# A mixer's first norm applied to the projections' results, and the modulation's loads behind the compression's

## The chip, the cores and the metric

One core of one Trainium2 chip runs the whole program. The metric is the device time of one execution in microseconds. The engines are named as the profile names them: PE is TensorE (PEld its loading of weights), DVE is VectorE, ACT is ScalarE, POOL is GpSimd, SP is the engine whose queue issues nearly all DMA transfers here.

## The reference, cut to what matters

The program is one block of a language model (a mixer of sparse attention and linear attention, then a mixture of 32 experts) followed by two layers of a second block that is modulated by two vectors c and c_ctx. What the change touches stands at the start of the first block and in the modulation of the second:

```python
u = rms_norm(h, g_mix)              # x * rsqrt(mean(x * x) + EPS) * g, row by row (256 rows of 1024)
z = u @ w_in                        # 4904 columns: q, k and v of the sparse attention, its gate,
                                    # q, k, v, a low-rank gate and r of the linear attention, two mixing gates
k_cmp = compress_blocks(k_c, cmp_pos_k, cmp_w1_k, ...)   # gelu(flat @ w1 + b1) @ w2 + b2; the same for v
o = o * rsqrt(mean(o * o) + EPS) * norm_g                # of the linear attention, per head
o = o * silu(r)
...
mod = silu(c) @ ada_w[layer] + ada_b[layer]              # second block, two layers, ada_w is 1024 x 3072
mod_c = silu(c_ctx) @ ada_w[layer] + ada_b[layer]
```

The factor rsqrt(mean + EPS) of the norm, called r1 below, is one number for each row of h, so u @ w_in is r1 times (h * g) @ w_in.

## The kernel before

All data are float32; most products are made as three products of halves: a matrix is split into hi (rounded to fp32r by ScalarE) and lo (the rest, subtracted by VectorE or, for every fourth part, by GpSimd), and gmm (L308) issues hi*hi, hi*lo and lo*hi (named after their tiles in the trace: m<-whi,uhi, m<-wlo,uhi, m<-whi,ulo, all L315). Tokens are held as 2 tiles of 128 rows, u transposed as 8 tiles (k) of 128 x 256.

The weights of the projections come through Feed (L178 on): chunks of 256 columns (the first of 280, the fourth of 272) are loaded by SP into three buffers, one called w (every third chunk), two called wst; a buffer is loaded again as soon as its last part is split. A chunk is split in four parts, into five pairs of buffers whi and wlo. The order of the chunks is Z_ORDER (5, 6, 7, 8, 2, 9, 10, 3, 4, 0, 1). Results go to two banks of PSUM called m; a chunk of more than 256 columns takes both.

TensorE's instructions run in the order in which they are written; the other engines' order is made by a scheduler. To write TensorE's order, the parts of the mixer are generators which drive (L144) interleaves by costs and delays that they yield: gla (linear attention), compress, mixer_proj (the projections), and behind them, as a background stream, ada (the modulation). A stream that waits for a name goes on when another has added it to done.

mixer_in (L490) turns h into four banks t, makes the norm's factor from the sums of squares (Newton steps, rsqrt, L352), turns it into a row R for all partitions (turn_rows, L445), and makes u from the banks: a product with g_mix and R on VectorE, hi on ScalarE, lo on GpSimd (L504 to L507). g_mix stands in VT, which VectorE copies at the start. rope_tables makes cos and sin and their copies times 0.125 for q. mixer_proj (L594) takes the results of each chunk out of PSUM, for the most part with one activation on ScalarE; chunk 5, the first, gives the gate (a tanh) and a part of gqk.

we_load (L377) and we_tile (L384) hand out four buffers called we, 1 MB each, in turn, for the modulation's weights (24 loads of ada_w, pieces of 512 x 512), for the compression's first weights w1 (two halves for keys, two for values) and later for the experts'. A load into a buffer waits until what was in it is multiplied. ada (L1468) loads one piece ahead: in each step it issues the next load, then the four matmuls of the piece at hand (L1502, s<-we,scT), then lets ADA_PACE ns pass in drive's account. compress multiplies w1 at L704 (t<-we,mt).

## Time and profile before

| | us |
|---|---|
| median of 3 runs | 1238.26 |
| lowest, highest | 1237.36, 1241.32 |
| the profiled execution | 1239.08 |
| its span | 1237.3 |
| TensorE busy | 1114.7 (90%) |
| VectorE, ScalarE, GpSimd busy | 562.3, 453.3, 192.2 |

The mixer of the first block runs to about 276 us, the routing to about 300, the experts to about 850, the rest is the second block. The rows further down are copied from the page of the profile and from answers on its trace. A row of a timeline has the start in us, the length in us, engine, line, operation, output<-input and a count of merged instructions; in brackets how long the engine stood idle before it and what ended that. SPq is SP issuing a DMA; its length is that of issuing alone.

### The profile page before, as it was taken

The page shows a single profiled execution, that of the slowest core. Times are in us where ns is not written, and L with a number is a line of the kernel's source. Part 1 is how long each engine was busy: PE and PEld are TensorE (multiplying, and loading weights), DVE is VectorE, ACT ScalarE, POOL GpSimd, SP SyncE. Part 2 cuts the span into 40 slices and gives each one's busy share as a digit, 9 for nine tenths or more (in the row PEclk, how much of TensorE's full clock was granted, in tenths as well). Part 3 has the DMA queues.
Part 4 walks back from the last instruction along what each step waited for, and adds up shares of the span by engine and source line. Part 5 has one row for each costly group of instructions (what it writes and reads, how often), then busy time and mean ns, then how long its engine had stood idle before and what let it go on. Part 6 is the DMA issues. An engine that isn't in the chain of part 4 may idle for free. (4 is left out here: it accounts for less than half of the span.)

```text
span 1237.3 us, 19978 instructions
## 1 busy us (share of the span) xinstructions
PE 1114.7 (90%) x7855; PEld 793.0 (64%) x7855; DVE 562.3 (45%) x1401; ACT 453.3 (37%) x1109; POOL 192.2 (16%) x210
## 2 busy tenths in 40 slices
PE   5999999998989998788989899856989997899996
PEld 4868877784635654433456365512877787899996
DVE  5367773553131212423212300103697668776776
ACT  4534554531012101322210200103567553776663
POOL 6134012111000000000000000000311225325231
PEclk9999999997999999999999999998999998999999
DMA  7897659963999999999999999998535156465331
GB/s 251 281 305 258 205 181 334 342 254 144 358 409 388 374 379 376 409 407 403 409 354 399 401 344 370 388 407 303 167 107 163 56 136 144 132 154 132 110 117 64
DMA packets 181562, 337.64 MB, mean 273 GB/s; under 512 B 20053, under 2 KB 113306, under 8 KB 181466
## 3 DMA queue, kind: packets, MB, share of 16 engines
q1 hardware_dynamic: 179946, 333.78, 75.7%
q0 software_dynamic: 1104, 2.45, 0.7%
q8 instruction: 63, 1.03, 0.3%
q14 instruction: 33, 0.27, 0.1%
q10 hardware_dynamic: 416, 0.10, 0.0%
HBM read 331.58 MB, written 4.73 MB: 272 GB/s over the span
## 5 line engine op out<-in xcount | busy, mean ns | idle before, releaser
L1396 PE MATMUL g<-we,xg 128*32 128x512 f32 x624 | 109.8, 613 | 19.8 <-DMA we<-in_w_gate_dram 9.4
L318 ACT ACTIVATE whi<-wst 128x512 fp32r<-128x512 f32 (+1 forms) x158 | 98.4, 629 | 74.7 <-PE m L315 69.1
L218 DVE TENSOR_TENSOR wlo<-wst,whi 128x512 fp32r<-128x512 f32 (+2 forms) x119 | 93.9, 796 | 64.2 <-ACT whi L318 63.6
L315 PE MATMUL m<-whi,uhi 128*128 128x256 f32 (+2 forms) x368 | 109.8, 298 | 2.6 <-ACT uhi L318 1.9
L315 PE MATMUL m<-wlo,uhi 128*128 128x256 f32 (+2 forms) x368 | 105.9, 288 | 2.6 <-POOL wlo L218 2.6
L315 PE MATMUL m<-whi,ulo 128*128 128x256 f32 (+2 forms) x368 | 105.8, 287 | 0.0
L315 PE MATMUL s<-cuT,wst 128*128 128x256 f32 (+1 forms) x368 | 85.6, 385 | 0.7 <-ACT cuT L318 0.7
L315 PEld LDWEIGHTS s<-cuT,wst 128*128 128x128 f32 (+1 forms) x368 | 64.9, 183 | 27.9 <-issue 17.2
L315 PEld LDWEIGHTS m<-whi,uhi 128*128 128x128 f32 x368 | 71.5, 194 | 12.9 <-issue 5.8
L218 POOL TENSOR_TENSOR wlo<-wst,whi 128x512 fp32r<-128x512 f32 (+1 forms) x39 | 52.2, 1339 | 175.9 <-ACT whi L318 134.9
L218 POOL TENSOR_TENSOR wlo<-w,whi 128x512 fp32r<-128x512 f32 (+4 forms) x21 | 28.0, 1334 | 326.0 <-ACT whi L318 291.7
L315 PE MATMUL m<-xhi,whi 128*128 128x256 f32 x256 | 75.6, 295 | 0.0
L315 PEld LDWEIGHTS m<-wlo,uhi 128*128 128x128 f32 x368 | 71.5, 194 | 2.9 <-POOL wlo L218 2.8
L315 PE MATMUL m<-xhi,wlo 128*128 128x256 f32 x256 | 72.4, 283 | 0.0
L315 PE MATMUL m<-xlo,whi 128*128 128x256 f32 x256 | 72.3, 283 | 0.0
L315 PEld LDWEIGHTS m<-whi,ulo 128*128 128x128 f32 x368 | 71.5, 194 | 0.3 <-POOL ulo L507 0.3
L1396 PEld LDWEIGHTS g<-we,xg 128*32 128x32 f32 x624 | 22.6, 111 | 74.2 <-issue 36.3
L318 ACT ACTIVATE whi<-w 128x512 fp32r<-128x512 f32 (+4 forms) x82 | 50.9, 628 | 34.3 <-PE m L315 29.7
L324 DVE SCALAR_TENSOR_TENSOR eo<-d,STw,eo 128x512 fp32r<-128x512 f32 x16 | 12.0, 748 | 99.8 <-ACT eo L318 99.8
L1424 PE MATMUL d<-we,hT 128*32 128x512 f32 x272 | 49.3, 600 | 7.5 <-DMA we<-in_w_down_dram 6.8
L315 PE MATMUL s<-wst,cuT 128*128 128x256 f32 (+1 forms) x256 | 55.1, 366 | 0.0
L315 PEld LDWEIGHTS s<-wst,cuT 128*128 128x128 f32 x256 | 44.5, 196 | 14.2 <-issue 9.2
(613 smaller groups left out, 2520.3 us busy)
## 6 DMA issues: line engine op xcount, KB each, us to landing
we<-in_w_down_dram SPq DMA_DIRECT2D x40, 1024.0 KB
we<-in_w_gate_dram SPq DMA_DIRECT2D x39, 1024.0 KB
we<-in_w_up_dram SPq DMA_DIRECT2D x39, 1024.0 KB
we<-in_ada_w_dram SPq DMA_DIRECT2D x24, 1024.0 KB
wst<-in_c_in_w_dram SPq DMA_DIRECT2D x19, 1024.0 KB
wst<-in_ab_in_w_dram SPq DMA_DIRECT2D x14, 1024.0 KB
wst<-in_w_in_dram SPq DMA_DIRECT2D x13, 1024.0 KB
w<-in_w_up_dram SPq DMA_DIRECT2D x10, 1024.0 KB
```

The source lines that it names most:

```text
L218: (net.nc.gpsimd if pool else net.nc.vector).tensor_tensor(b, src, a, OP.subtract)
L315: mm(out, l, r, start=first and i == 0, stop=last and i == len(ps) - 1, skip_group_check=True)
L318: return self.nc.scalar.activation(out, in_, f, **kw)
L324: return self.nc.vector.scalar_tensor_tensor(out, a, s, b, op0=op0, op1=op1, **kw)
L1396: nc.tensor.matmul(b[32 * e:32 * e + 32, :], xg[:, 2 * j + r, 32 * e:32 * e + 32], v[e // 2][:, e % 2, 512 * r:512 * r + 512], start=j == ...
L1424: nc.tensor.matmul(ds[hf][32 * e:32 * e + 32, :], hT[:, k, 32 * e:32 * e + 32], v[e // 2][:, e % 2, 512 * hf:512 * hf + 512], start=k == 0 ...
```

## The change

Four things:

- mixer_in makes hi directly from the banks t, as h times g_mix (an activation with a scale), and lo as one scalar_tensor_tensor on VectorE; R is gone. The norm's factor is computed in a function of its own, norm1, that is called after the first chunk's matmuls are written; r1 and r1h (half of it) are scales of the activations that take the projections' results out of PSUM. rope_tables is called after the second chunk's matmuls and makes tables times r1 (ccr, sinr). For chunks 9 and 10 (r of the linear attention) silu leaves r1 out, and gla multiplies the factors of its norm by r1 instead.
- compress adds the name w1 once all four loads of its first weights are written.
- ada's first load is behind a wait for w1; it was the first thing that ada did.
- ADA_PACE is 6000 instead of 7500.

```diff
@@ -44,7 +44,7 @@
 UNIT_Q = 5000
 LANES = 3
 NSA_GAP = 0
-ADA_PACE = 7500
+ADA_PACE = 6000
 ROUTE = 3000
 MAGIC = 12582912.0
 HALVES = [(slice(0, 64), slice(64, 128)), (slice(64, 128), slice(0, 64))]
@@ -492,21 +492,27 @@
         b = self.bank(self.pm, "s", 1)
         nc.tensor.transpose(b[:, :8], self.vr[0:8], self.ident[0:8, 0:8])
         self.copy(self.VT[:, 0:8], b[:, :8])
+
         bs = [self.turn_h(k2, 5) for k2 in range(4)]
+        hi = self.t(A, [128, KD, 256], "uhi", dt=F32R)
+        lo = self.t(A, [128, KD, 256], "ulo", dt=F32R)
+        for k in range(KD):
+            s, g = bs[k // 2][:, 256 * (k % 2):256 * (k % 2) + 256], self.vcol("g_mix", k)
+            self.act(hi[:, k], s, AF.Copy, scale=g)
+            self.stt(lo[:, k], s, g, hi[:, k], OP.mult, OP.subtract)
+        self.uT = (hi, lo)
+
+    def norm1(self):
+
+        A = self.A
         xs = self.t(A, [128, 2, D], "mt1")
         ss = self.t(A, [128, 2], "r1ss")
         self.act(xs[:, 0], self.h[:, 0], AF.Square, accum_out=ss[:, 0:1])
         self.stt(xs[:, 1], self.h[:, 1], 1.0, self.h[:, 1], OP.mult, OP.mult, accum_out=ss[:, 1:2])
-        R = self.turn_rows(A, self.rsqrt(A, ss, 2, 1.0 / D), "r1rb", 5)
-        hi = self.t(A, [128, KD, 256], "uhi", dt=F32R)
-        lo = self.t(A, [128, KD, 256], "ulo", dt=F32R)
-        for k in range(KD):
-            t = xs[:, k // 4, 256 * (k % 4):256 * (k % 4) + 256]
-            self.stt(t, bs[k // 2][:, 256 * (k % 2):256 * (k % 2) + 256], self.vcol("g_mix", k), R, OP.mult, OP.mult)
-            self.act(hi[:, k], t)
-            self.nc.gpsimd.tensor_tensor(lo[:, k], t, hi[:, k], OP.subtract)
-        self.uT = (hi, lo)
-        self.rope_tables(self.K)
+        self.r1 = self.t(A, [128, 2], "r1")
+        self.r1h = self.t(A, [128, 2], "r1h")
+        self.copy(self.r1, self.rsqrt(A, ss, 2, 1.0 / D))
+        self.ts(self.r1h, self.r1, 0.5)
 
     def rope_tables(self, A):
         nc = self.nc
@@ -532,8 +538,15 @@
         self.sin = sin
         self.ccq = self.t(A, [128, 2, 64], "ccq")
         self.sinq = self.t(A, [128, 2, 32], "sinq")
-        self.ts(self.ccq, self.cc, 0.125)
-        self.ts(self.sinq, sin, 0.125)
+
+        self.ccr = self.t(A, [128, 2, 64], "ccr")
+        self.sinr = self.t(A, [128, 2, 32], "sinr")
+        for i in range(2):
+            r = self.r1[:, i:i + 1]
+            self.ts(self.ccr[:, i], self.cc[:, i], r)
+            self.ts(self.sinr[:, i], sin[:, i], r)
+        self.ts(self.ccq, self.ccr, 0.125)
+        self.ts(self.sinq, self.sinr, 0.125)
 
     def rope_half(self, out1, out2, ps, nh, cc, sin, pool):
 
@@ -604,7 +617,12 @@
         self.sr = self.t(A, [128, 2, 512], "sr")
         for ci in Z_ORDER:
             yield from self.proj_tok(self.uT, W_IN[ci][1])
+            if ci == Z_ORDER[0]:
+                self.norm1()
+            if ci == Z_ORDER[1]:
+                self.rope_tables(self.K)
             for i, ps in enumerate(self.res):
+                r, rh = self.r1[:, i:i + 1], self.r1h[:, i:i + 1]
                 if ci < 2:
                     s = slice(4 * ci, 4 * ci + 4)
                     self.rope_half(self.qr[:, i, s, 0:32], self.qr[:, i, s, 32:64],
@@ -612,29 +630,30 @@
                                    self.ccq[:, i], self.sinq[:, i], self.K)
                 elif ci == 2:
                     self.act(self.kcd[:, i], ps.rearrange("p (a d) -> p a d", d=64)[:, :, None, :]
-                             .to_broadcast([128, 4, 2, 64]))
+                             .to_broadcast([128, 4, 2, 64]), scale=r)
                 elif ci in (3, 4):
                     br = ci - 3
                     kd_ = self.ksr[:, i, br]
                     self.rope_half(kd_[:, :, 0:32], kd_[:, :, 32:64],
                                    ps[:, 0:128].rearrange("p (h d) -> p h d", d=64), 2,
-                                   self.cc[:, i], self.sin[:, i], self.K)
-                    self.act(self.vsw[:, i, br], ps[:, 128:256])
+                                   self.ccr[:, i], self.sinr[:, i], self.K)
+                    self.act(self.vsw[:, i, br], ps[:, 128:256], scale=r)
                 elif ci == 5:
-                    self.act(self.gate[:, i], ps[:, 0:24], AF.Tanh, scale=0.5)
+                    self.act(self.gate[:, i], ps[:, 0:24], AF.Tanh, scale=rh)
                     self.ts(self.gate[:, i], self.gate[:, i], 0.5, 0.5, OP.mult, OP.add)
-                    self.act(self.gqk[:, i, 0:256], ps[:, 24:280])
+                    self.act(self.gqk[:, i, 0:256], ps[:, 24:280], scale=r)
                 elif ci == 6:
-                    self.act(self.gqk[:, i, 256:512], ps)
+                    self.act(self.gqk[:, i, 256:512], ps, scale=r)
                 elif ci == 7:
-                    self.act(self.gv[:, i, 0:256], ps)
+                    self.act(self.gv[:, i, 0:256], ps, scale=r)
                 elif ci == 8:
-                    self.act(self.gv[:, i, 256:512], ps[:, 0:256])
-                    self.act(self.ga[:, i], ps[:, 256:272])
+                    self.act(self.gv[:, i, 256:512], ps[:, 0:256], scale=r)
+                    self.act(self.ga[:, i], ps[:, 256:272], scale=r)
                 else:
                     o = self.sr[:, i, (ci - 9) * 256:(ci - 8) * 256]
                     th = self.t(A, [128, 256], "th", 1)
-                    self.act(th, ps, AF.Tanh, scale=0.5)
+
+                    self.act(th, ps, AF.Tanh, scale=rh)
                     self.stt(o, th, 1.0, ps, OP.add, OP.mult)
             self.done.add("z%d" % ci)
         self.dump("gqk", self.gqk)
@@ -645,7 +664,7 @@
             for j in range(4):
                 yield from self.proj_tok(self.uT, 256)
                 for i, ps in enumerate(self.res):
-                    self.act(self.mt[br][:, i, 256 * j:256 * j + 256], ps, AF.Tanh, scale=0.5)
+                    self.act(self.mt[br][:, i, 256 * j:256 * j + 256], ps, AF.Tanh, scale=self.r1h[:, i:i + 1])
             if br:
 
                 for half in range(2):
@@ -696,6 +715,8 @@
             for hf in range(2):
                 w1.append((yield from self.we_load(I["cmp_w1_" + n][0][1024 * hf:1024 * hf + 1024]
                                                    .rearrange("(k p) n -> p k n", p=128), 8, 256)))
+            if kv:
+                self.done.add("w1")
             yield (0, 4000)
             b = self.bank(pm, "t", 5)
             for hf, (v, tag) in enumerate(w1):
@@ -1011,6 +1032,8 @@
                 self.act(junk, b[:, 128 * h:128 * h + 128], AF.Square, accum_out=ssq[:, 4 * i + h:4 * i + h + 1])
             yield 2200
         y = self.rsqrt(G, ssq, 8, 1.0 / 128, "rg")
+        for i in range(2):
+            self.ts(y[:, 4 * i:4 * i + 4], y[:, 4 * i:4 * i + 4], self.r1[:, i:i + 1])
         for i in range(2):
             for h in range(4):
                 hs = slice(128 * h, 128 * h + 128)
@@ -1475,7 +1498,6 @@
                 self.I["ada_w_2"][l][512 * hf:512 * hf + 512, 512 * c:512 * c + 512]
                 .rearrange("(k p) n -> p k n", p=128), 4, 512)))
         todo = [(l, c, hf) for l in range(2) for c in range(6) for hf in range(2)]
-        yield from load()
 
         scT = self.t(A, [128, KD, 42], "scT")
         nc.gpsimd.memset(scT, 0.0)
@@ -1489,6 +1511,8 @@
             self.act(th[:, r], self.vcol(n, 0, 8), AF.Tanh, scale=0.5)
             self.stt(th[:, r], th[:, r], 1.0, self.vcol(n, 0, 8), OP.add, OP.mult)
             self.ts(scT[:, :, 10 + r], th[:, r], 0.5)
+        yield from self.wait("w1")
+        yield from load()
         for l in range(2):
 
             sums = self.bank(self.pm, "s", 1)
```

What this makes of the engines' order, at three places. First VectorE at the start, behind the copy of VT (rs.. are the norm's steps, mt is the product that becomes u, wlo the first weights' low half, w their buffer). Before:

```order
L321 TENSOR_TENSOR rsa<-rsa,rsx 128x2
L324 SCALAR_TENSOR_TENSOR rsy<-rsa,rsy 128x2
L332 COPY r1rb<-rsy 128x256
L218 TENSOR_TENSOR wlo<-w_93,whi 128x560
L324 SCALAR_TENSOR_TENSOR mt_137<-t,VT,r1rb 128x256 x8
L218 TENSOR_TENSOR wlo<-w_93,whi 128x560 x2
```

After:

```order
L324 SCALAR_TENSOR_TENSOR ulo<-t,VT,uhi 128x256
L324 SCALAR_TENSOR_TENSOR rsy<-rsa,rsy 128x2
L321 TENSOR_TENSOR rsa<-rsy 128x2
L321 TENSOR_TENSOR rsa<-rsa,rsx 128x2
L324 SCALAR_TENSOR_TENSOR ulo<-t,VT,uhi 128x256 x6
L218 TENSOR_TENSOR wlo<-w_93,whi 128x560
L324 SCALAR_TENSOR_TENSOR ulo<-t,VT,uhi 128x256
L218 TENSOR_TENSOR wlo<-w_93,whi 128x560 x2
L218 TENSOR_TENSOR wlo<-wst,whi 128x512 x2
L324 SCALAR_TENSOR_TENSOR rsy<-rsa,rsy 128x2
```

The first wlo stood ahead of the eight products, and now stands behind seven of the eight lo; the end of the norm's chain has moved behind the first chunk's splits. ScalarE, in the same way, has seven of the eight hi ahead of the first whi; before, two whi stood ahead of the first hi.

Second SP, which issues the loads in this order (w and wst from in_w_in are chunks of the projections, we the modulation's ada_w and the compression's w1, called cmp_w_k and cmp_w_v). Before:

```order
L431 DMA tab<-in_table_dram 128x1424
L386 DMA we<-in_ada_w_dram 128x4x512
L394 DMA w_271<-in_w_in_dram 128x8x272
L394 DMA wst<-in_w_in_dram 128x8x256 x2
...
L386 DMA we<-in_cmp_w_k_dram 128x8x256
L386 DMA we<-in_ada_w_dram 128x4x512
L394 DMA w_817<-in_w_in_dram 128x8x256
L386 DMA we<-in_cmp_w_v_dram 128x8x256 x2
L386 DMA we<-in_ada_w_dram 128x4x512 x3
```

After:

```order
L431 DMA tab<-in_table_dram 128x1424
L394 DMA w_209<-in_w_in_dram 128x8x272
L394 DMA wst<-in_w_in_dram 128x8x256 x2
...
L386 DMA we<-in_cmp_w_v_dram 128x8x256
L394 DMA w_776<-in_w_in_dram 128x8x256
L386 DMA we<-in_ada_w_dram 128x4x512 x5
L394 DMA wst<-in_w_in_dram 128x8x256
```

The first modulation load was ahead of the fourth chunk's; now it stands behind all four of w1 and behind the tenth chunk's (w_817 before, w_776 after).

Third TensorE where the compression multiplies the keys' w1 (L704 before, L725 after; la and gqk belong to the linear attention). Before:

```order
L925 MATMUL t<-tab,la 128x256 x2
L1502 MATMUL s<-we,scT 32x512 x4
L704 MATMUL t<-we,mt_235 32x256 x8
L437 MATMUL t<-tab,gqk 128x128 x4
L947 MATMUL t<-la,tab 128x256
L704 MATMUL t<-we,mt_235 32x256 x8
```

After:

```order
L946 MATMUL t<-tab,la 128x256 x2
L725 MATMUL t<-we,mt_173 32x256 x16
L437 MATMUL t<-tab,gqk 128x128 x4
L968 MATMUL t<-la,tab 128x256
L1526 MATMUL s<-we,scT 32x512 x4
```

The modulation piece before this place was the fourth; the one after it is the first, and the buffer of its weights is the one that the first eight matmuls of L725 read.

## Rows read from the trace of the kernel before

**Rows 1.** Busy time by stretch (us; instructions), then TensorE's granted clock, DMA share, GB/s:

```profile
16.00:276.00 260.00, 251.82 (x2054) 209.00 (x2054) 150.56 (x379) 129.54 (x325) 64.34 (x66) 0.99 0.79 270
...
20.00:30.00 10.00, 7.38 (x46) 6.96 (x46) 4.85 (x7) 4.49 (x9) 6.95 (x6) 0.84 0.74 271
...
130.00:140.00 10.00, 10.00 (x74) 9.03 (x73) 7.33 (x28) 4.95 (x21) 0.00 (x0) 0.83 0.38 123
...
280.00:290.00 10.00, 7.98 (x33) 7.01 (x34) 5.94 (x34) 3.60 (x9) 0.26 (x1) 0.52 0.29 107
```

**Rows 2.** Timeline of TensorE, the first chunk (280 columns) and the second:

```profile
16.25 0.60 PE L315 MATMUL m<-whi,uhi 128*128 128x280 f32 x1 [1.89 <-ACT uhi L318]
...
17.46 0.44 PE L315 MATMUL m<-whi,uhi 128*128 128x280 f32 x1
17.69 0.44 PE L315 MATMUL m<-wlo,uhi 128*128 128x280 f32 x1
...
22.72 0.29 PE L315 MATMUL m<-whi,ulo 128*128 128x280 f32 x1
22.85 0.29 PE L315 MATMUL m<-whi,uhi 128*128 128x280 f32 x1
25.76 0.40 PE L315 MATMUL m<-wlo,uhi 128*128 128x280 f32 x1 [2.62 <-POOL wlo L218]
...
27.68 0.58 PE L315 MATMUL m<-whi,uhi 128*128 128x256 f32 x1
```

**Rows 3.** Timeline of ScalarE, the same stretch:

```profile
10.47 0.67 ACT L318 ACTIVATE whi<-w 128x560 fp32r<-128x560 f32 x1
...
16.66 1.32 ACT L318 ACTIVATE uhi<-mt 128x256 fp32r<-128x256 f32 x4
...
23.69 1.28 ACT L318 ACT_TABLE_LOAD   x1
27.16 0.19 ACT L318 ACTIVATE gate<-m 128x24 f32<-128x24 f32 x1 [2.19 <-PE m L315]
27.25 0.38 ACT L318 ACTIVATE gqk<-m 128x256 f32<-128x256 f32 x1
```

**Rows 4.** Timeline of VectorE, the same stretch:

```profile
10.48 0.16 DVE L332 COPY VT<-s 128x8 f32<-128x8 f32 x1
...
13.52 0.73 DVE L218 TENSOR_TENSOR wlo<-w,whi 128x560 fp32r<-128x560 f32 x1
14.81 3.23 DVE L324 SCALAR_TENSOR_TENSOR mt<-t,VT,r1rb 128x256 f32<-128x256 f32 x8 [0.55 <-ACT r1rb L318]
```

**Rows 5.** Timeline of GpSimd, the same stretch:

```profile
16.28 8.11 POOL L507 TENSOR_TENSOR ulo<-mt,uhi 128x256 fp32r<-128x256 f32 x8 [5.41 <-ACT uhi L318]
24.35 1.36 POOL L218 TENSOR_TENSOR wlo<-w,whi 128x560 fp32r<-128x560 f32 x1
```

**Rows 6.** Timeline of TensorE: compression, start of window attention, first experts:

```profile
71.37 1.07 PE L1502 MATMUL s<-we,scT 128*32 128x512 f32 x8
72.25 1.05 PE L704 MATMUL t<-we,mt 128*32 128x256 f32 x16
73.23 0.66 PE L437 MATMUL t<-tab,gqk 128*128 128x128 f32 x4
...
74.25 1.07 PE L704 MATMUL t<-we,mt 128*32 128x256 f32 x16
...
83.01 1.07 PE L704 MATMUL t<-we,mt 128*32 128x256 f32 x16 [0.64 <-DMA we<-in_cmp_w_v_dram]
...
126.92 1.09 PE L437 MATMUL t<-tab,PT 128*128 128x128 f32 x8 [0.85 <-DVE PT L321]
...
307.89 1.48 PE L1396 MATMUL g<-we,xg 128*32 128x512 f32 x10 [0.34 <-DMA we<-in_w_up_dram]
```

**Rows 7.** Timeline of SP, the issues of two of those stretches:

```profile
70.51 0.37 SPq L394 DMA_DIRECT2D w<-in_w_in_dram  x1
...
299.66 2.88 SPq L1354 DMA_DIRECT2D we<-in_w_up_dram  x4
```

**Rows 8.** The page, part 2: GB/s moved in 40 equal slices of the span:

```profile
GB/s 251 281 305 258 205 181 334 342 254 144 358 409 388 374 379 376 409 407 403 409 354 399 401 344 370 388 407 303 167 107 163 56 136 144 132 154 132 110 117 64
```

## The prediction

> **What bounds the kernel now.** I read the profile from the stage that the change touches outwards: first the busy time of the engines from 16 to 276 us, then TensorE's rows in order of time, then the engines that it waits for. TensorE (PE) is busy for 251.8 of these 260 us, at 0.99 of the full clock, VectorE (DVE) for 151, the DMA engines for 0.79 of the time [rows 1]. So the mixer is bound by TensorE: work that only moves inside it costs nothing, and only three things can change its end: when the first projection starts, where TensorE stands idle, and what clock it is granted. What follows it (routing, the experts' weights, the second block) starts from its end, so I take a shift of the mixer's end as a shift of the whole.
>
> The start: the first projection matmul begins at 16.25, waiting for the first part of u; the fourth stands at 17.46, the next at 17.69, 0.23 us apart; later in the same chunk 0.13 [rows 2]. The clock is thus at its lower level, 1.2 GHz, until about 20. At 25.76 TensorE has stood idle for 2.62 us, for the fourth split of the first weights on GpSimd (POOL), and the second chunk begins at 27.68 [rows 2]. In the stretch 20 to 30 the granted clock is 0.84 [rows 1]: 3.2 us of it run at the lower level, behind that idle time.
>
> **The change part by part.**
>
> *The first norm behind the first chunk.* Today VectorE copies VT at 10.48, does the norm's chain, one wlo at 13.52, and from 14.81 eight products, 0.40 us each (3.23 for 8) [rows 4]. ScalarE then makes hi from them, and POOL lo: 8.11 us for eight, until 24.4, with the late split behind them [rows 5]. After: hi is made from PSUM as soon as VT is there. On ScalarE seven hi stand ahead of the first split; at 0.33 each (1.32 for four) from 10.7 they end at 13.0, the split (0.67) at 13.7 [rows 3]. That is 2.5 us before today's first matmul, but the second matmul needs wlo, and VectorE has seven lo ahead of it. From VT at 10.48 to the wlo at 13.52 it does twenty small instructions in 3.04 us, 0.15 each [rows 4]; after, twelve of them and one lo (0.40) stand ahead of the other six: 10.6 + 1.8 + 0.4 = 12.8 at most, six lo to 15.1, wlo 0.73: 15.8. From there the matmuls run without a break; the fourth starts at about 16.3 instead of 17.46. If the clock rises at 20 as today, 16 more are through by then, and 28 are left, at 0.13 each: the chunk is through at 23.6. POOL's split, free of the eight lo, takes 1.36 us from about 15.9 [rows 5]: the idle 2.62 us are gone, and the buffer comes free 8 us earlier, so that SP issues the fourth chunk's load 8 us earlier too, with no modulation load ahead of it. What is late next: the second chunk needs the bank that ScalarE reads, and there the fourth split of the second weights (it waits for a buffer of matmul 36, at 22.1; 0.6 us), the table load (1.28) and 0.5 for gate and gqk stand in a row [rows 3]: 24.6. So the second chunk starts at 24.6 instead of 27.68: **-3.1** (-3.6 with an earlier rise of the clock, -1.5 with one 2.5 us later). The idle time left, 1 us, is shorter than the one that cost the clock, so I take the 3.2 us at the lower level as gone, of which 0.3 lie in the first chunk: **-1.4** (0 if they return).
>
> *r1 on the results.* The scale of an activation is an operand of an instruction that is there already; six small operations on VectorE for the rope tables, two for r1 and two for gla's factors are new, some 2 us at 0.2 each, while VectorE is busy for 151 of 260 us [rows 1]. Nothing waits for them: r1 is due at 23.9, and stands ahead of the third wlo of the second chunk, at about 20.9. Zero.
>
> *The modulation's weights behind w1.* TensorE's work for the 24 pieces stays, 0.88 us each (71.37 to 72.25) [rows 6]. Today the first pieces are loaded long before use, at 19 us the first. After, the compression's four loads take the four buffers of "we", and the first modulation load waits until the first half of the keys' w1 is multiplied. In TensorE's order its use comes soon behind: the second half (0.98, as 72.25 to 73.23), four transposes and one matmul (1.02, to 74.25) [rows 6]. That is 2.0 us of cover. What is queued behind it on TensorE is everything. A load of 1 MB is not that fast: of four issued from 299.66 the second released TensorE at 307.89, 8.2 us after the first was issued [rows 6, 7]. At the fastest slice of the page, 409 GB/s [rows 8], 1.05 MB take 2.6 us, so one alone takes some 5.6 (an estimate from these rows). Just ahead of it on SP stands the projection's load that was issued at 70.51, and TensorE ends the first half of w1 about 1.9 us behind that (71.37 without the piece, plus 0.98) [rows 6, 7]: so 8.2 - 1.9 = 6.3 us from issue, and a wait of 6.3 - 2.0 = **+4.3** (3.6 alone in the queue; 5.7 if the load before it is as late as the second of the four).
> The Trainium skill ("DMA: Bandwidth & Descriptors", Anatomy of one DMA) states for the other issuing path about 2 us fixed and the bytes at 436 GB/s; worked out for this load that is an estimate of 4.4 us. By it the wait would be 2.4 and the total 1238.6; the row at 307.89 speaks for the longer one.
>
> *The clock behind that wait.* 2.62 us of idle time were followed by 3.2 us at the lower level [rows 1, 2]; behind 4.3 us I take the same, half of it lost: **+1.6** (0 if it falls into the wait itself; 3.4 for two such stretches, as 280 to 290 stays at 0.52 [rows 1]).
>
> *What else moves.* The values' w1 are now loaded early: the wait of 0.64 at 83.01 goes, **-0.6** [rows 6]. The linear attention's chain before 70 loses two pieces of 0.88 that stood under its waits and gets six projection matmuls (0.7): **+0.5** (0 to 0.9). At the start of the window attention TensorE waits 0.85 for PT on VectorE [rows 6], with two pieces ahead of it; one is left, so the wait grows by its 0.88: **+0.9** (0 to 0.9). On SP five modulation loads now stand ahead of the eleventh projection load; the fifth waits for the first piece's product, while three projection chunks lie loaded ahead: zero. The pace (7500 to 6000) lets the last piece end a dozen matmuls later, still ahead of the router's logits: zero.
>
> Sum: -3.1 - 1.4 + 4.3 + 1.6 - 0.6 + 0.5 + 0.9 = +2.2 us. The profiled execution took 1239.08 (span 1237.3 and 1.8 around it), 0.8 above the median 1238.26; against the median that is **1240.5**, a change too small for this kernel's measurement (0.3%, 3.7 us, is about what it can tell from none).
>
> **The rivals.**
> *Slower: the clock stays down.* With the start's idle time (13.9 to 15.8 and 1 us at 23.6) and the long wait at the first modulation piece, the clock is granted at half for two stretches more than I count, as around 276 to 290, where waits of one to two us keep it at 0.52 [rows 1]. Each costs 1.6 us: +1.6 at the second chunk (the -1.4 does not come) and +1.7 behind the piece: +5.3, 1243.6. It decides from one such stretch on: +2.2 + 1.6 is over 0.3%. For it: the wait of 0.85 at 126.92 [rows 6] stands ahead of a stretch granted 0.83 [rows 1], though the work there is also of small matmuls. Against: the start's 1 us is well under the 2.62 that cost the clock before.
> *Faster: the first modulation load is hidden.* Should its load be issued early enough (a buffer of "we" free before w1 is multiplied, or TensorE itself late for another reason), the wait and its clock go: +2.2 - 4.3 - 1.6 = -3.7, 1234.6. Against it: four buffers, four loads of w1 ahead, and the order on SP.
> *More modulation pieces wait.* The second and third load follow 1 and some 8 us behind the first, and at 0.79 DMA busy [rows 1] each MB ahead costs 2.6 us; one more wait of that size gives +4.8, 1243.1. Against: their uses lie 5 us and more behind one another.
> *The norm does not shorten the start.* If the first wlo is later than 15.8 by VectorE's order, at worst by the three products left behind it (1.2 us), the gain is -1.9 instead of -3.1: +3.4, 1241.7.
>
> **How the numbers follow.** My forecast, one wait at the first piece with one stretch at the lower clock, and the start as worked out, with a start that gains or not: 0.53. Clock: 0.20. More waits: 0.12. Hidden: 0.15, of which two thirds end beyond -0.3%, since the start can also gain 0.5 more. Slower by over 0.3% (above 1242.0) gets the clock and the further waits, 0.32, and 0.01 of the forecast's own upper end; faster 0.10; within 0.3% the other 0.57. The range reaches from the hidden load with part of its wait to the clock case: 1235.5 to 1244.0.
>
> **What would show it.** Right: the fourth projection matmul near 16.3, the second chunk at 24 to 25, no wait for POOL near 25; one wait of 3.6 to 5.7 us on L1526 for a DMA of ada_w at 65 to 75 us and a lower clock behind it; no wait on the values' w1; the routing's start 1 to 4 us later than today. Wrong: no wait at L1526, or several; a half clock at 25 to 30 again; a different length of the experts' stage, which I take to move as one piece.

## The result: slower by 8 us, and the profile after

| us | before | after |
|---|---|---|
| median (4 runs each) | 1238.82 | 1246.99 |
| lowest, highest | 1237.36, 1241.32 | 1246.36, 1247.81 |
| the profiled execution, its span | 1239.08, 1237.3 | 1247.81, 1246.0 |
| TensorE busy | 1114.7 | 1121.7 |
| first product behind the mixer | 277.95 | 284.25 |

The ratio is 1.0064 (95% interval 1.0046 to 1.0082); a second measurement beside more runs of the kernel before gave 1247.32 against 1238.42, 1.0080 (1.0064 to 1.0096). The forecast was 1240.5 with a range of 1235.5 to 1244.0: the sign is right, the size is not, and the time lies above the range.

TensorE in the profile after, in order of time (the columns are those of [rows 2]; it answers to [rows 2] and [rows 6]):

```profile
14.96 0.60 PE L315 MATMUL m<-whi,uhi 128*128 128x280 f32 x1 [3.11 <-ACT whi L318]
15.74 0.60 PE L315 MATMUL m<-wlo,uhi 128*128 128x280 f32 x1 [0.17 <-DVE wlo L218]
...
24.90 0.39 PE L315 MATMUL m<-whi,uhi 128*128 128x256 f32 x1 [1.14 <-ACT gqk L318]
...
59.49 0.32 PE L982 MATMUL t<-qs,kt 128*32 128x64 f32 x8 [0.97 <-DVE kt L321]
...
65.96 1.93 PE L725 MATMUL t<-we,mt 128*32 128x256 f32 x32
67.83 0.66 PE L437 MATMUL t<-tab,gqk 128*128 128x128 f32 x4
68.32 0.60 PE L968 MATMUL t<-la,tab 128*128 128x256 f32 x2
72.66 1.07 PE L1526 MATMUL s<-we,scT 128*32 128x512 f32 x8 [3.74 <-DMA we<-in_ada_w_dram]
...
127.40 2.35 PE L437 MATMUL t<-tab,PT 128*128 128x128 f32 x16 [2.16 <-DVE PT L321]
...
284.25 0.66 PE L437 MATMUL s<-tab,vc 128*128 128x128 f32 x2 [1.34 <-DVE lg L324]
```

The start came as worked out: the second matmul at 15.74, the second chunk at 24.90 instead of 27.68, and no wait for GpSimd. So did the new wait, 3.74 us at L1526 for ada_w. At PT, where 0.85 us were waited for [rows 6], 2.16 are now. The same stretches by TensorE's granted clock (columns as in [rows 1]):

```profile
20.00:30.00 10.00, 8.87 (x72) 8.64 (x71) 4.95 (x19) 5.99 (x11) 1.27 (x1) 1.00 0.83 284
70.00:80.00 10.00, 7.34 (x70) 5.35 (x74) 4.47 (x14) 0.63 (x1) 3.92 (x4) 0.83 0.79 282
125.00:135.00 10.00, 7.84 (x57) 7.26 (x55) 7.67 (x18) 3.96 (x13) 0.86 (x2) 0.83 0.57 200
145.00:155.00 10.00, 10.00 (x83) 8.52 (x80) 6.05 (x20) 4.97 (x21) 0.00 (x0) 0.83 0.50 188
```

The lower clock behind the start's idle time is gone (1.00, was 0.84 [rows 1]). It stands now in three places: behind the wait at L1526, around PT (where the kernel before had one too, in 130 to 140 [rows 1]), and near 149, where TensorE never stood idle. The mixer ends 6.3 us later. The remaining 2.4 us of the spans' difference (8.7) lie behind it; 2 of them belong to this one execution, as the second profile of the changed kernel shows below.

### The profile page after: what moved, and what is told of

The parts are those of the page before. It is cut to its first block, busy times and chain, and to the rows that moved or that the text cites. A ratio compares the mean times of both kernels' runs of the same rounds, so it can differ in the third digit from the quotient of the medians.

```text
span 1246.0 us, 19977 instructions
## 1 busy us (share of the span) xinstructions
PE 1121.7 (90%) x7853; PEld 797.6 (64%) x7853; DVE 563.8 (45%) x1408; ACT 457.4 (37%) x1108; POOL 184.0 (15%) x202
```

## The experiments

All times are medians with the kernel before measured beside them. "Mixer's end" is the start of the first product with vc in the run's own profile, one execution. That execution can lie far from its run's median: in e5_early_load it was the slowest of twelve (1246.50), in e7_start the fastest (1234.90). e3_late_use, c_late and c_late2 are one kernel, called the base below.

| run | us (runs) | before beside it | ratio, interval | mixer's end |
|---|---|---|---|---|
| c_after: the changed kernel again | 1247.32 (6) | 1238.42 | 1.0080, 1.0064 to 1.0096 | 284.27 |
| c_before: the kernel before again | 1238.51 (1) | 1238.42 | | 277.92 |
| e1_norm: norm's part alone | 1242.85 (12) | 1238.24 | 1.0040, 1.0018 to 1.0062 | 284.44 |
| e2_wait: modulation's part alone | 1248.57 (6) | 1238.24 | 1.0082, 1.0053 to 1.0111 | 285.87 |
| e5_early_load: first load early | 1240.82 (12) | 1238.42 | 1.0022, 1.0010 to 1.0033 | 280.80 |
| e3_late_use: first piece later | 1237.86 (12) | 1238.24 | 0.9996, 0.9978 to 1.0013 | 276.42 |
| c_late: e3 again | 1239.17 (12) | 1238.25 | 1.0000, 0.9982 to 1.0018 | 276.91 |
| c_late2: e3 again | 1237.79 (12) | 1238.58 | 0.9991, 0.9979 to 1.0003 | 276.14 |
| e6_old_norm_late: e3's modulation, old norm | 1238.57 (12) | 1238.42 | 1.0000, 0.9987 to 1.0014 | 279.52 |
| c_old_late2: e6 again | 1240.13 (12) | 1238.58 | 1.0013, 1.0000 to 1.0026 | 279.03 |
| e8_pt_bare: e3, a piece less ahead of PT | 1239.84 (12) | 1238.25 | 1.0007, 0.9991 to 1.0024 | 278.85 |
| e7_start: e3, earlier start | 1241.31 (12) | 1238.25 | 1.0018, 0.9999 to 1.0037 | 278.30 |
| e9_best: e7, a piece more at PT | 1242.86 (12) | 1238.25 | 1.0023, 0.9999 to 1.0047 | 282.45 |
| e10_start2: e3, another early start | 1237.81 (12) | 1238.58 | 0.9991, 0.9976 to 1.0005 | 276.74 |
| e11_start3: e3, a third | 1239.04 (12) | 1238.71 | 0.9996, 0.9977 to 1.0015 | 277.93 |

**The two kernels again.**

> The changed kernel again, beside the next runs and on their chip: 1247 us against 1238 to 1239. Theory A (the loss hangs on the one long wait and the clock behind it) expects the wait of 3.7 us at the first modulation piece and the half clock right behind it again; the half clocks near 129, 149 and 1061 us may stand elsewhere or be missing, and the time differ by some 2 us for each. If these three stand at the same places again, they belong to the kernel and not to the single execution.

> The kernel before, profiled again: TensorE's waits as in the first profile (2.6 us near 26, 0.6 at the values' w1, 0.85 at PT), and behind the wait near 26 a half clock of 3.4 us. Whether the half clock near 133 us stands there again tells whether it belongs to the kernel.

The mixer's end repeats to 0.03 us in both kernels, 277.95 and 277.92 against 284.25 and 284.27: the 6.3 us belong to the change. In the changed kernel the wait was 3.75, PT 2.16, and the three stretches of 70 to 80, 125 to 135 and 145 to 155 were granted 0.83 again. In the kernel before the lower clock near 133 was not there again (130 to 140 was granted 1.00), but one in 140 to 150 (0.83), where the first profile had 1.00. So not all of these stretches are the kernel's. The clearest case is behind the mixer, in 1060 to 1070, where TensorE has stood idle for 4.5 us in either execution. The first profile of the changed kernel:

```profile
1060.00:1070.00 10.00, 9.30 (x39) 8.33 (x39) 7.90 (x28) 5.67 (x18) 1.27 (x1) 0.53 0.56 183
```

The second:

```profile
1060.00:1070.00 10.00, 8.95 (x54) 8.10 (x55) 9.36 (x32) 7.14 (x23) 1.26 (x1) 0.83 0.56 183
```

39 matmuls against 54 in the same 10 us: the granted clock after the same idle time was 0.53 once and 0.83 once. That is the 2 us of the first pair of profiles, and it comes and goes; one execution of one kernel may lie 3 us off another for such reasons (c_late2: 1235.03 to 1240.41).

**Which part loses.** The first run takes the changed kernel's norm with the modulation as before, the second the reverse.

```diff
 # e1_norm, against the changed kernel
-ADA_PACE = 6000
+ADA_PACE = 7500
         todo = [(l, c, hf) for l in range(2) for c in range(6) for hf in range(2)]
+        yield from load()
...
-        yield from self.wait("w1")
-        yield from load()
 # e2_wait, against the kernel before
-ADA_PACE = 7500
+ADA_PACE = 6000
...
+            if kv:
+                self.done.add("w1")
...
         todo = [(l, c, hf) for l in range(2) for c in range(6) for hf in range(2)]
-        yield from load()
...
+        yield from self.wait("w1")
+        yield from load()
```

> The norm's part of the change alone: the modulation's first load and the pace of 7500 are as in the kernel before. Theory A (the start gains, the modulation's part loses): only the start's two terms are left, about 2.8 us from the second chunk starting at 24.9 instead of 27.68 and 1.4 us from the half clock behind it, so 4.2 us less than before: about 1234.6 us, no half clock between 25 and 32 us, no wait of TensorE for ada_w, PT waited for as long as before (0.85 us). Theory B (the norm's part itself costs, by r1 in the linear attention's chain and by the later loads; the modulation's part is innocent): 1241 us or more. Either may be shifted by up to 2 us if the half clock behind the idle time near 1054 us is longer or shorter when everything before it moves.

> The modulation's part alone: the norm is that of the kernel before, the first modulation load waits for the four w1 loads, pace 6000. Theory A: 3.7 us for the wait of TensorE at the first piece, 2.0 for the half clock behind it, 1.3 more at PT, less 0.6 at the values' w1, and about 0.5 for the linear attention's chain: 6.9 us over before, 1245.7 us, with a half clock at 25 to 30 as before. Theory B: the modulation's part is innocent, 1238 to 1240 us. A third reading (the two parts only lose together, because the norm's earlier start moves TensorE's work ahead of the loads): between 1239 and 1243 us, with a wait at the first piece under 2 us.

Either part alone is slower. The modulation's part costs what theory A gave and 3 us more, with 3.90 us of wait at its first piece. The norm's part alone should have gained 4.2 by theory A and loses 4.6; theory B has the number, but not the place that it named. TensorE of that run at the values' w1:

```profile
79.90 1.07 PE L725 MATMUL t<-we,mt 128*32 128x256 f32 x16 [1.44 <-DMA we<-in_cmp_w_v_dram]
82.81 1.93 PE L725 MATMUL t<-we,mt 128*32 128x256 f32 x16 [1.83 <-DMA we<-in_cmp_w_v_dram]
```

and the ten us around them, by busy time and granted clock:

```profile
80.00:90.00 10.00, 8.17 (x57) 6.29 (x57) 0.69 (x1) 1.83 (x6) 0.00 (x0) 0.60 0.93 337
```

The second half of w1 is released at 82.81, in the kernel before at 83.01 [rows 6]. SP issued the two loads 3.0 us earlier than in the kernel before. SP in the norm-only run:

```profile
69.44 2.46 SPq L386 DMA_DIRECT2D we<-in_cmp_w_v_dram  x2
```

SP in the kernel before:

```profile
72.49 1.23 SPq L386 DMA_DIRECT2D we<-in_cmp_w_v_dram  x2
```

They landed no earlier, with the DMA engines busy for 0.93 of the stretch. So in the old order the 3 us by which TensorE came earlier are waited away by 83, in two pieces instead of one, and the clock falls to 0.60 over the next ten us: 0.2 us ahead of the kernel before at 82.81, this run is 4.1 behind it at its next modulation piece (95.54 against 91.44). This execution then had another stretch of lower clock (0.66 in 150 to 160); it lies 3.9 above its run's median, so the 4.1 fit the 4.6 of the medians better than the mixer's end does. The change's two parts belong together: moving the modulation's loads behind w1 is what lets w1 come early (no wait at L725 in the changed kernel).

**The wait at the first piece.** Two ways to take it away. The first keeps TensorE's instructions in exactly the same order and swaps two loads, the second shifts the pieces.

```diff
 # e5_early_load, against the changed kernel
-            if kv:
-                self.done.add("w1")
+                if kv and not hf:
+                    self.done.add("w1")
+                    yield 0
 # e3_late_use, against the changed kernel
-ADA_PACE = 6000
+ADA_PACE = 5700
         yield from load()
+        yield (0, 6000)
```

> The changed kernel with TensorE's instructions in exactly the same order, but the first modulation load takes the place in the queue of the fourth w1 load, which comes behind (its use is some 13 us later). Only the wait at the first piece can go. Theory A by my terms: 3.7 us of wait and 2.0 of clock, 1247.0 - 5.7 = 1241.3 us. If the wait brings more half clocks later than the one behind it (as the run with the later first piece suggests, which gained 9): 1238 to 1240 us. Rival (what gained there was not the wait but the other places of the pieces and the pace): 1245 us or more. PT should be waited for as long as in the changed kernel, 2.2 us, as its cover is the same.

> The changed kernel with one edit: in the account that orders TensorE the first modulation piece comes 6000 ns after its load instead of right behind, which puts it behind 18 projection matmuls, parts of the linear attention and the first half of the values' w1 (pace 5700, so that the last piece stands where it stood). The load itself is issued as before. Theory A: the wait of 3.7 us at the first piece and the half clock behind it (2.0) go: 1247.0 - 5.7 = 1241.3 us, no wait for ada_w over 0.5 us, granted clock 1.0 from 72 to 80 us. Rival: the wait only moves on to the next piece or to PT, or the half clock comes back elsewhere: 1245 us or more.

TensorE of the run with the early load:

```profile
66.84 1.93 PE L726 MATMUL t<-we,mt 128*32 128x256 f32 x32
68.71 0.66 PE L437 MATMUL t<-tab,gqk 128*128 128x128 f32 x4
69.20 0.60 PE L969 MATMUL t<-la,tab 128*128 128x256 f32 x2
69.73 1.07 PE L1527 MATMUL s<-we,scT 128*32 128x512 f32 x8
...
123.76 3.47 PE L437 MATMUL t<-tab,PT 128*128 128x128 f32 x16 [2.16 <-DVE PT L321]
```

No idle time ahead of L1527, and 70 to 80 granted 1.00. The median falls by 6.5 us (1247.32 to 1240.82, measured side by side), where theory A gave 5.7; the intervals of the two ratios lie apart. Since TensorE's order is the same, this is what the wait and all that came of it cost. The traces locate 4.6 of it: at the values' w1 this run is 3.6 us ahead of c_after (76.13 against 79.75) although its second chunk came 1.0 later (25.79 against 24.82), which makes the wait of 3.75 and 0.8 for the clock behind it. The other 2 us are not located; the profiled execution is the slowest of this run, and around PT it was at the lower clock for longer (125 to 135 granted 0.71, in c_after 0.83). PT is waited for 2.16 us as in the changed kernel, as expected. The later first piece goes below what theory A gave, 1237.9 where 1241.3 was expected; what it has and the early load has not is a second piece ahead of PT, and other places for the other pieces.

**PT.** The edit gives one piece a longer gap and the next a shorter one, so that one of the two ahead of PT comes behind it.

```diff
 # e8_pt_bare, against e3_late_use
-                    yield (930, ADA_PACE if c < 5 or not hf else 1000)
+                    yield (930, ADA_PACE + {(0, 2, 0): 2000, (0, 2, 1): -2000}.get((l, c, hf), 0) if c < 5 or not hf else 1000)
```

> The same as the run with the later piece, but of the two modulation pieces ahead of the products with PT at the start of the window attention one comes behind them. Theory A (a piece there covers VectorE's work on PT, and its absence also costs clock): PT is waited for 2.2 us instead of 0.84, and a half clock of 3.4 us stands behind it: 1.3 + 1.1 = 2.4 us more, about 1240.3. Rival (the wait there is covered or made good in what follows): within 1 us, 1237 to 1239.

TensorE with the piece moved behind:

```profile
117.86 1.97 PE L437 MATMUL t<-tab,PT 128*128 128x128 f32 x16
121.98 3.50 PE L437 MATMUL t<-tab,PT 128*128 128x128 f32 x16 [2.16 <-DVE PT L321]
...
278.85 1.66 PE L437 MATMUL s<-tab,vc 128*128 128x128 f32 x8 [1.48 <-issue]
```

TensorE with two pieces ahead (c_late2):

```profile
118.67 1.97 PE L437 MATMUL t<-tab,PT 128*128 128x128 f32 x16
121.48 1.09 PE L437 MATMUL t<-tab,PT 128*128 128x128 f32 x8 [0.85 <-DVE PT L321]
122.84 1.06 PE L437 MATMUL t<-tab,PT 128*128 128x128 f32 x8 [0.26 <-DVE PT L321]
...
276.14 1.94 PE L437 MATMUL s<-tab,vc 128*128 128x128 f32 x8 [1.48 <-issue]
```

The wait grows by 1.31, the 16 products behind it take 3.50 us instead of 2.4, and the mixer ends 1.9 to 2.7 us later than in the three profiles of the base. 120 to 135 was granted 0.89 (1.00 in the base). Not all of that is PT's: 140 to 150 was granted 0.83 too, in the base 1.00. The medians differ by 0.7 only (1239.84 against 1239.17), which this spread can't tell from 2.4 or from zero: the longer wait is shown in the trace, its size in the time is not. The stretch of lower clock at PT stood in all five profiles with 2.16 us of wait (twice in the changed kernel, the modulation's part alone, the early load, this one); with 0.85 it stood in three of eleven (the first profile of the kernel before, e6 and e7, but not, for one, in the second of the kernel before, where 125 to 135 and 130 to 140 were granted 1.00). It stood once with hardly any wait: e9_best waited 0.18 there and was granted 0.83 in 125 to 135. So the wait of 2.16 goes with the lower clock here, but is not its only occasion.

**What the norm is worth.** The base with the old norm, measured first apart from the base, then beside it.

> The norm of the kernel before with the modulation of the run with the later first piece (load behind w1, first piece 6000 ns later, pace 5700). Against that run it lacks the norm's part alone, with no wait for ada_w in either. Theory A: the start's gain of 2.8 us and the half clock of 1.4 behind 26 us come back, 1237.9 + 4.2 = 1242.1 us. Rival (the start's gain is lost later whatever the loads do, since DMA or VectorE set the pace at 60 to 90 us): within 1.5 us of that run, 1237 to 1239.5.

> The run with the later first modulation piece again, as the base of the three beside it and as a second reading of what the norm's part is worth: 1237.9 us if the first reading holds (the same modulation with the old norm took 1238.6, in another call).

> The run with the later first modulation piece, third reading, now in one call with the same modulation under the old norm. Theory A (the start's gain reaches the end): 2.5 to 3 us less than that. Rival (it is lost behind the mixer): within 1 us of it.

> The old norm with the same modulation: mixer's end about 279.5 us as before. Theory A: about 1241 if the run beside it takes 1238; rival: the same time.

Measured apart, the medians differed by 0.6 or 0.7, once in favour of either, while the mixer's end differed by about 3 us (279.52 against 276.42). Side by side it is 1240.13 against 1237.79: 2.3 us, with intervals that just overlap (1.0000 to 1.0026, 0.9979 to 1.0003), and 279.03 against 276.14 in the traces. But little of these 3 us is the start's. The second chunk comes 2.4 later with the old norm (27.37 against 24.94), the first product with PT 0.9 (119.61 against 118.67); 2 more are added behind it, by a stretch of lower clock that only c_old_late2 had. Old norm:

```profile
140.00:150.00 10.00, 10.00 (x65) 7.62 (x65) 6.28 (x18) 3.95 (x18) 0.00 (x0) 0.66 0.39 148
```

The base, c_late2:

```profile
140.00:150.00 10.00, 9.49 (x84) 7.10 (x80) 7.56 (x26) 6.41 (x24) 0.45 (x1) 1.00 0.61 211
```

Such a stretch is not the old norm's: e6_old_norm_late was granted 1.00 there, and e11_start3, with the new norm, 0.67. Between e6_old_norm_late and e3_late_use the first product with PT lies 2.2 apart (121.15 against 118.96); e6 had the lower clock behind the wait for GpSimd (0.84 in 20 to 30), and c_old_late2 did not have it. In these two pairs the norm's part is thus worth 0.9 us up to PT, and 2.2 with the clock behind the start; c_late, a base whose first chunks came later, reached PT at 119.48 and would make it 0.1 and 1.7. What is left of it in the time is not settled, by these medians something between nothing and 2.3 us. And the old norm with the late modulation, where nothing waits for ada_w, is itself at 1.0000 and 1.0013, its mixer's end 1.1 to 1.6 us behind that of the kernel before: moving the pieces late gains nothing by itself, and may cost something.

**An earlier start.** Three tries to get more of it, on top of the base: the first two hi and lo of u ahead of the first split, six behind; in the second and third the gate taken out of PSUM by VectorE, ahead of ScalarE's table load. They differ in where the norm's chain stands on VectorE.

```diff
 # e10_start2, against e3_late_use (e7_start: norm1 where it was, gate as it was;
 # e11_start3: without the stt on ss; e9_best: e7_start and a third piece between the products with PT)
+        V2 = self.V2 = self.t(A, [128, 8], "VT2")
         for k in range(KD):
-            s, g = bs[k // 2][:, 256 * (k % 2):256 * (k % 2) + 256], self.vcol("g_mix", k)
+            if k == 2:
+                self.feed.split()
+                w0 = self.feed.two[0][0]
+                self.stt(V2, w0[:, 0, 0:8].bitcast(F32), 0.0, self.VT[:, 0:8], OP.mult, OP.add)
+            s = bs[k // 2][:, 256 * (k % 2):256 * (k % 2) + 256]
+            g = self.vcol("g_mix", k) if k < 2 else V2[:, k:k + 1]
...
+            if k == 2:
+                self.norm1()
...
+        self.stt(ss, self.V2[:, 0:2], 0.0, ss, OP.mult, OP.add)
...
-            if ci == Z_ORDER[0]:
-                self.norm1()
...
-                    self.act(self.gate[:, i], ps[:, 0:24], AF.Tanh, scale=rh)
-                    self.ts(self.gate[:, i], self.gate[:, i], 0.5, 0.5, OP.mult, OP.add)
+                    self.ts(self.gate[:, i], ps[:, 0:24], rh)
                     self.act(self.gqk[:, i, 0:256], ps[:, 24:280], scale=r)
+                    if i:
+                        self.act(self.gate, self.gate, AF.Tanh)
+                        self.ts(self.gate, self.gate, 0.5, 0.5, OP.mult, OP.add)
```

> The same with an earlier start: the first two hi and lo of u stand ahead of the first split of the weights, the other six behind it on ScalarE and VectorE (they read a copy of g_mix that is made once the first split is there), and the norm's chain stands behind the first splits. Only the order at the start changes. The second projection matmul should come near 13.2 us instead of 15.9 and the second chunk near 22.5 instead of 24.9. Theory A (the start is worth what it shows in the trace): 2.4 us less than the run with the later piece, about 1235.5. Rival (what the start gains is given back later, at loads or at VectorE): within 1 us of it, 1237 to 1239.

> The run with the later piece and a start that doesn't give back what it gains: as in the first kernel with an earlier start (two hi and lo of u ahead of the first split, six behind), but the norm's chain starts right behind the first split, and the gate is taken out of PSUM by VectorE, its tanh coming later, so that ScalarE's table load doesn't stand between the first chunk's end and the second chunk. Expected in the trace: second projection matmul near 13.6 us, first chunk through at 20.4, second chunk at about 22 (25.2 to 25.8 in the run beside it), no half clock at 25 us. Theory A: 3 to 3.5 us less than the run beside it, about 1235. Rival (the start's gain is lost behind the mixer, or comes back as half clock): within 1 us of it.

> The run with the later piece, two hi and lo of u ahead of the first split and six behind it, the gate taken out of PSUM by VectorE ahead of the table load, and the norm's chain where VectorE has time for it, ahead of the first wlo. Expected in the trace: second projection matmul near 15 us, the factor r1 at about 14.5 and so no wait for it, second chunk at about 23 instead of 25, TensorE idle ahead of it for less than 1.2 us and no half clock at 25. Theory A (what the start gains reaches the end as long as no idle time over 2 us is made): 2 us less than the run with the later piece, about 0.8 + 2 = 2.8 us under the kernel before beside it, 1235.6. Rival: within 1 us of the kernel before.

> The earlier start, and a third modulation piece between the products with PT, where 0.84 us are still waited for. Theory A: 0.8 us less than the run with the earlier start, about 1234.7, and 3.5 us less than the kernel before. Rival: as in the run with the earlier start, the gain is given back, 1237 or more.

TensorE at the second chunk in e10_start2:

```profile
21.24 0.28 PE L315 MATMUL m<-whi,ulo 128*128 128x280 f32 x1
24.03 0.58 PE L315 MATMUL m<-whi,uhi 128*128 128x256 f32 x1 [2.51 <-ACT gqk L318]
```

ScalarE there:

```profile
23.51 0.47 ACT L318 ACTIVATE gqk<-m,r 128x256 f32<-128x256 f32 x1 [2.79 <-DVE gate L328]
```

The first chunk ends at 21.5, but the factor r1 is there only at 22.9: its results, and with them the bank, wait for the norm that was put behind. 2.51 us of idle time, and 20 to 30 is granted 0.83 (1.00 in the base). In e7_start the same place waits 3.47. With the chain early (e11_start3) the second matmul is at 15.12 and the second chunk at 24.19 with 0.46 us of idle time, 0.7 to 1.6 ahead of the base; that is under what the medians can tell, the mixer's end is behind the base's (277.93, with 0.67 granted in 140 to 150), and the times show nothing. e9_best made a wait of 2.02 us at 163 for the modulation's own sums (t<-tab,apart), by the order of its pieces, and lost there more than it gained at PT (0.18 waited, 0.84 to 0.85 in the base); 160 to 170 was granted 0.83, and 20 to 30 0.68 behind a wait of 3.06 at the second chunk. None of these beats both kernels beyond its interval; the lowest, c_late2 and e10_start2, stand at 0.9991 with 1 in the interval.

## Why the prediction was wrong

Point by point, in its own terms:

- **The start, -3.1 and -1.4.** This is the step that failed. In the trace it is nearly as forecast up to the second chunk (-2.8) and in the clock behind it (1.00). But the text carried both terms to the end in full, and the runs with the old norm, against the base, show 0.9 left at PT (c_old_late2), and 2.2 where the old start had its lower clock (e6_old_norm_late). That clock is not a fixed debt either: in c_old_late2, which has the old start, the wait for GpSimd was 1.94 us, and no lower clock followed it (1.00 from 24 to 32). Where the rest of the start's gain goes between the second chunk and PT stays open; two waits near 40 take a little of it (0.55 and 0.35 with the new norm in c_late2, 0.37 and 0.18 with the old in c_old_late2).
- **The first modulation load, +4.3 and +1.6.** The mechanism was right, place, releaser and consequence. 3.74 us of wait; with what came of it 6.5 in the medians against 5.9 forecast, 4.6 of it located in the traces. The sum used the row of the load that released TensorE 8.2 us after the issue of the first of four; this load took 5.57, issue at 67.09 to 72.66, which is the lower bound that the text worked out as 5.6. SP in the profile after:

```profile
64.73 0.37 SPq L394 DMA_DIRECT2D w<-in_w_in_dram  x1
67.09 15.05 SPq L386 DMA_DIRECT2D we<-in_ada_w_dram  x5
```

  The projection's load ahead of it was 2.4 us old by then and added nothing. The estimate of 4.4 us from the Trainium skill ("DMA: Bandwidth & Descriptors", Anatomy of one DMA), whose figures are for the other issuing path, was 1.2 below the row's 5.57; the lower bound from the rows was the better guide here.
- **The values' w1, -0.6.** Right: no wait at L725. What the text left unsaid is that the start's gain needs this part of the change. Its row [rows 6] shows that TensorE came 0.64 us before these loads; with the old order of loads and an earlier start it comes still earlier, and the norm-only run waits 3.27 us for them.
- **PT, +0.9.** Undersized. The text counted the piece that is missing as cover. The wait grew by 1.31, not 0.88, and at 2.16 us a stretch of lower clock followed it in every profile, which the text considered for the first piece and not here. What this costs in the time is not shown: e5's median lies some 2.5 us above those of the base, but was not measured beside them and has other places for its pieces; e8's, which was, lies 0.7 above, with 1.9 to 2.7 in its trace.
- **The linear attention, +0.5.** Wait 0.97 for 0.37, +0.6: right. But it was the only place where the late pieces were given a price for standing elsewhere. With the old norm and no wait for ada_w the mixer still ends 1.1 to 1.6 us later than in the kernel before, some of it in waits of 0.3 to 0.5 more at other places (0.64 for 0.36 at the linear attention's r, near 100), the rest not located; the medians show nothing once (1.0000) and 1.6 us the other time (1.0013).
- **What is left.** The lower clock near 149 stood in both profiles of the changed kernel, with TensorE busy throughout, and not in the three of the base. But seven of the 17 profiles have such a stretch beginning between 140 and 151, with no idle time of one us in the ten us ahead of it, among them the kernel before (c_before), the old norm with the late modulation (c_old_late2) and e11_start3. Its cause stays open. That stretch, and 2 us behind the mixer that the medians have and c_after's trace has not, stand in no term of the sum.

Put together by medians: the base stands at 0.9991 to 1.0000 of the kernel before. The forecast for it by the same terms, without the wait, its clock and the missing piece at PT, would have been 2.2 - 4.3 - 1.6 - 0.9 = -4.6 us: of that gain nothing is left. The loss, from the base (1238.3 over its three medians) to the changed kernel (1247.3), is 9.0 where the terms made 6.8: 6.5 of it goes with the wait (e5), the other 2.5 lies between e5 and the base and can't be told apart into PT and the places of the other pieces. So the larger part of the miss of 6 to 7 us is the gain, 4 to 5 of it, and the smaller one the loss. Why the base gains nothing is shown in part only: the start's gain shrinks on the way, and late pieces bring none.

The rival that came nearest is "the clock stays down", 1243.6, but at other places than it named, and together with the further terms above. The range was too narrow for that: it took the rivals one at a time, and it made no room for what one execution differs from the next.

## What to carry to other kernels

A stage whose loads arrive just in time has no use for an earlier start: look at the first wait for a DMA behind it, and count the gain only up to there. When work is moved off a queue's front, see what it covered at each place that it leaves, and what it is released by where it goes; both are to be read from the order and the waits before the change. From 20 us to the mixer's end the 17 profiles have 16 idle times of TensorE of 2.0 us and more (2.02 to 3.90), and each was followed by a stretch at 1.2 GHz, so give such a wait its price with the clock, and not by its length alone. But about as many stretches stood there without such an idle time ahead of them, and they came and went between executions of one kernel: look at more than one profile before you put a lower clock down to a change.

## What was not expected of the hardware

- The same idle time of 4.5 us before the same matmuls was followed by a granted clock of 0.53 in one execution and 0.83 in the other, over ten us: 39 matmuls against 54.
- TensorE was granted 0.83 in 145 to 155 in both profiles of the changed kernel without any idle time there, and in one of two of the kernel before in 140 to 150; with the old norm and the late modulation 0.66 in 140 to 150 in one profile and 1.00 in the other.
- Twelve runs of one kernel lay between 1235.0 and 1240.4 us, and two medians of twelve of the same kernel 1.4 apart (1237.79 and 1239.17). A difference of 2 us can be told only with both kernels measured side by side, and then barely.
- Two loads of 1 MB issued 3.0 us earlier were released at 82.81 instead of 83.01, with the DMA engines busy for 0.93 of that stretch.
